# Unpinning the matmul engine's instruction order in a two-layer decoder trunk

## The chip, the cores and the metric

The kernel runs on one core of one Trainium2 chip. The metric is the device time of one execution in microseconds (us); smaller is better. The time before is the median of three runs.

## The reference

The reference is a trunk of two layers over 256 tokens of width 2048 in float32. Each layer computes

```
h = rms_norm(x, norm_mix);  proj = h @ w_in            # columns shared out among three groups of heads
A: 4 heads of differential attention (two softmax maps a head, subtracted, then an RMS norm per head)
B: 6 heads of softmax attention with a running forget gate added to the logits
C: 6 heads of latent attention (q and kv go through low-rank products first)
x = x + concat(A, B, C) @ w_out
x = x + square(relu(rms_norm(x, norm_ffn) @ w_ff_up)) @ w_ff_down      # 8192 wide
```

All heads are causal, with q and k normalised per head. With 256 tokens there are two blocks of 128 rows.

## The kernel before

**Weights.** Every weight matrix is streamed from HBM once, in tiles of 128 rows by up to 1024 columns. `load_w` loads a tile into `wraw` (5 buffers), ScalarE (ACT) rounds it to `whi` (3 buffers) and VectorE (DVE) computes the rest `wlo` (3 buffers). Each product is a sum of three: activation high part by `whi`, activation low part by `whi`, activation high part by `wlo`. TensorE (PE) accumulates it in PSUM. A weight tile therefore is a burst of matmuls: 8 on `whi` and 4 on `wlo` in a projection, for instance.

**Stages of a layer.** First come the projection groups `mq`, `mkv`, `fv0`, `fq0`, `fk0`, `fv1`, `fq1`, `fk1`, `dq`, `dk`, `dv` (with the low-rank products `qup` and `kvup` behind `mkv`), then the output product `wo`, then the feed-forward products `u` (up) and `dn` (down) in blocks of 1024 hidden columns.

**Attention in the background.** The attention of a head is a generator: scale q and k on DVE, transpose them on PE (`qk`), copy to SBUF, scores on PE (`s`), mask, exp and normalise on DVE and ACT (`p`), transpose the probabilities on PE (`pt`), copy (`pT`), weighted values on PE (`o`), split into `mix`. The object `bg` (`Background`) holds these generators, and after every weight tile `bg.step()` advances them by 1.25 stages on average. So attention is interleaved by hand with the next group's weight tiles. For the differential heads, `diff_rotation` scales and rotates `dqk` on DVE, `diff_maps` makes two maps and their difference, and `diff_outputs` normalises `osb` and transposes it into the last four slots of `mix`. The first 12 of the 16 rows of `mix` heads are multiplied by the left half of `w_out` while this runs; `bg.finish()` then runs what is left, and the last four heads follow.

**Order of the work.** The tile framework orders each engine's instructions at compile time. It walks a timing estimate of its own; on each engine it takes, of the instructions whose inputs that estimate says are there and whose buffers are free, the one that stands earliest in the program. The chip then runs each engine's list in that order, and semaphores make an instruction wait for its inputs. DVE, ACT and the DMA queues are ordered so. PE is the exception: `mm` and `transpose_block` hand every matmul and transpose to `in_order`, which ties it behind the PE instruction traced just before it. PE's list is the program's own order:

```
def in_order(ins):
    tc.keep_in_program_order(ins)
def mm(out, lhsT, rhs, start, stop):
    in_order(nc.tensor.matmul(out, lhsT, rhs, start=start, stop=stop))
def transpose_block(dst, src):
    in_order(nc.tensor.transpose(dst, src, ident))
```

Score, transpose and value tiles share four PSUM buffers (`t_tile`); the accumulators of the projections have four others (`acc_tile`). The feed-forward blocks use the two sets in turn.

Of the kernel before, what the change touches and what calls it, by code (L numbers as in the profile page):

```python
# [125 lines left out]
def trunk_kernel(ctx: ExitStack, tc: tile.TileContext, ins: dict, out: bass.AP):  # L126
    nc = tc.nc
# [12 lines left out]
    def t_tile(name):  # L140
        return ps_t.tile([P, 512], F32, tag="t", name=name)


    def in_order(ins):
        tc.keep_in_program_order(ins)

    def mm(out, lhsT, rhs, start, stop):
        in_order(nc.tensor.matmul(out, lhsT, rhs, start=start, stop=stop))  # L148

    bg = Background()  # L150

# [16 lines left out]
    for _ in range(WARM):  # L168
        mm(warm, zeros[:, :P], zeros, True, True)
# [8 lines left out]
    ident, ones, upto = (cst[:, i * P:(i + 1) * P] for i in range(3))  # L178
# [50 lines left out]
    class FirstNorm:  # L229
# [33 lines left out]
        def scale(self):  # L263

            b = t_tile("ss")
            for t in range(NT):
                for i in range(2):
                    mm(b[:, t:t + 1], self.squares[:, i * SEQ + t * P:i * SEQ + (t + 1) * P], ones[:, 0:1], i == 0, i == 1)
            ss = sp.tile([P, NT], F32, tag="ssm", name=f"ss_{self.name}")
            nc.vector.tensor_copy(ss, b[:, :NT])  # L270
            return rsqrt_of(ss, NT, [(slice(0, NT), D_MODEL)], self.name)

    class Norm:
# [7 lines left out]
        def columns(self, c0, n):  # L281
            for q in range(c0 // 512, (c0 + n) // 512):
                for t in range(NT):
                    junk = sp.tile([P, 512], F32, tag="junk", name="junk")
                    nc.scalar.activation(junk, x[:, t, q * 512:(q + 1) * 512], AF.Square, accum_out=self.sums[:, t, q:q + 1])
            for k in range(c0 // P, (c0 + n) // P, 2):
                b = acc_tile("xt")
                for i in range(2):
                    for t in range(NT):
                        transpose_block(b[:, i * SEQ + t * P:i * SEQ + (t + 1) * P], x[:, t, (k + i) * P:(k + i + 1) * P])  # L290
                h = parts_tile("ht", "ht")
                for i in range(2):
                    split_to(h[:, i], b[:, i * SEQ:(i + 1) * SEQ], self.gain[:, k + i:k + i + 1])
                self.h.append(h)
                yield
# [7 lines left out]
    def product_t(acc, chunks, hi, lo, off, start, stop):  # L303


        for w in (hi, lo):
            for i, (c, j) in enumerate(chunks):
                wk = w[:, off + i * P:off + (i + 1) * P]
                if w is hi:
                    mm(acc, wk, c[:, j].rearrange("p a t -> p (a t)"), start and i == 0, False)  # L310
                else:
                    mm(acc[:, :SEQ], wk, c[:, j, 0, :], False, stop and i == len(chunks) - 1)
# [43 lines left out]


    def transpose_block(dst, src):
        in_order(nc.tensor.transpose(dst, src, ident))

    def scores(q_terms, k_terms, decay=None):

# [26 lines left out]
    def transposed_p(p):  # L389

        pt = t_tile("pt")
        for i in range(3):
            transpose_block(pt[:, i * P:(i + 1) * P], p[:, i * P:(i + 1) * P])
        pT = ap.tile([P, 3 * P], F32, tag="pT", name="pT", bufs=3)
        nc.scalar.copy(pT, pt[:, :3 * P])
        return pT
# [8 lines left out]
    def heads_transposed(pairs):  # L405

        b = t_tile("qk")
        for i, blocks in enumerate(pairs):
            for t in range(NT):
                transpose_block(b[:, i * SEQ + t * P:i * SEQ + (t + 1) * P], blocks[t])  # L410
        return b
# [14 lines left out]
    for l in range(DEPTH):  # L426
# [85 lines left out]
        for g in range(4):  # L512
            dst = mk if g < 2 else mv
# [468 lines left out]
def build(shapes):  # L982
    import concourse.bacc as bacc

    nc = bacc.Bacc("TRN2", target_bir_lowering=False, num_devices=1, dynamic_dma_scratch_size=1024)
    ins = {k: nc.dram_tensor(f"in_{k}", s, F32, kind="ExternalInput").ap() for k, s in shapes.items()}
    out = nc.dram_tensor("out_0", (SEQ, D_MODEL), F32, kind="ExternalOutput").ap()
    with tile.TileContext(nc) as tc:  # L988
        trunk_kernel(tc, ins, out)
    return nc  # L990
# [9 lines left out]
```

## Time and profile before

| what | value |
|---|---|
| median of 3 runs | 2188.17 us (2185.26 to 2188.57) |
| time of the profiled execution | 2187.5 us |
| its span, first to last instruction | 2185.7 us |
| instructions | 29225, of these 11080 matmuls or transposes on PE |
| PE busy | 2158.2 us, 99% of the span |
| mean granted TensorE clock | 0.996 |

PE is the row for matmuls and transposes, PEld the row for the weight loads of the same engine, which overlap the matmuls before them. Matmuls are pipelined, and their ends are modelled; an idle time of PE in a row is counted from the modelled end of the one before. A granted clock of 1.00 is 2.4 GHz, 0.5 is 1.2 GHz.

### The profile page before, as it was taken

How to read it: one execution, taken by the hardware profiler on the slowest of the kernel's cores; microseconds unless marked ns; L12 is line 12 of the kernel's file. 1: busy time of each engine (PE TensorE's matmuls, PEld its weight loads, DVE VectorE, ACT ScalarE, POOL GpSimd, SP SyncE). 2: the span in 40 equal slices, each digit the busy share in tenths (PEclk: the TensorE clock that was granted, in tenths of full speed). 3: DMA queues.
4: the chain of work that ended last, by engine and by line, in shares of the span. 5: the costliest groups of instructions: out<-in, count | busy, mean ns of one | idle time of the engine just before them, and what ended most of it. 6: DMA issues, size and time to landing. Idle time of an engine off the chain costs nothing. (4 is left out here: it accounts for less than half of the span.)

```text
span 2185.7 us, 29225 instructions
## 1 busy us (share of the span) xinstructions
PE 2158.2 (99%) x11080; PEld 1864.3 (85%) x11080; DVE 1359.8 (62%) x2160; ACT 1085.4 (50%) x1603; POOL 12.7 (1%) x16
## 2 busy tenths in 40 slices
PE   9999999999999999999999999999999999999999
PEld 7998778888888888888889997788888888888887
DVE  7876656665565555655568766666565655655554
ACT  6655445554444444444456554555444544444442
POOL 2000000000000000000000000000000000000000
PEclk9999999999999999999999999999999999999999
DMA  8545435555556665565655455455565566566664
GB/s 270 175 139 170 151 132 165 191 185 193 190 193 190 190 191 192 191 193 183 187 161 169 142 177 164 137 182 186 190 192 193 188 192 190 191 192 193 190 191 149
DMA packets 115421, 395.70 MB, mean 181 GB/s; under 512 B 13008, under 2 KB 13136, under 8 KB 115280
## 3 DMA queue, kind: packets, MB, share of 16 engines
q1 hardware_dynamic: 115280, 393.83, 56.7%
q8 instruction: 87, 1.43, 0.3%
q14 instruction: 54, 0.44, 0.1%
HBM read 391.68 MB, written 2.10 MB: 180 GB/s over the span
## 5 line engine op out<-in xcount | busy, mean ns | idle before, releaser
L199 DVE TENSOR_TENSOR wlo<-wraw,whi 128x1024 fp32r<-128x1024 f32 (+3 forms) x773 | 908.6, 1177 | 727.9 <-ACT whi L198 717.6
L198 ACT ACTIVATE whi<-wraw 128x1024 fp32r<-128x1024 f32 (+3 forms) x773 | 789.7, 1023 | 968.7 <-PE dn L148 361.9
L148 PE MATMUL u<-ht,whi 128*128 128x512 f32 x2048 | 513.0, 392 | 0.0
L148 PE MATMUL dn<-whi,g 128*128 128x512 f32 x2048 | 511.2, 390 | 0.9 <-ACT whi L198 0.4
L148 PEld LDWEIGHTS dn<-whi,g 128*128 128x128 f32 x2048 | 383.0, 188 | 82.0 <-DVE x L327 2.3
L148 PEld LDWEIGHTS u<-ht,whi 128*128 128x128 f32 x2048 | 369.1, 189 | 66.7
L148 PEld LDWEIGHTS u<-ht,wlo 128*128 128x128 f32 x2048 | 279.4, 190 | 20.0
L148 PE MATMUL u<-ht,wlo 128*128 128x256 f32 x2048 | 285.5, 282 | 0.0
L148 PE MATMUL dn<-wlo,g 128*128 128x512 f32 x1024 | 276.3, 389 | 0.0
L148 PEld LDWEIGHTS dn<-wlo,g 128*128 128x128 f32 x1024 | 192.2, 188 | 40.0
L148 PE MATMUL wo<-whi,mix 128*128 128x512 f32 x512 | 138.8, 403 | 0.3
L148 PEld LDWEIGHTS wo<-whi,mix 128*128 128x128 f32 x512 | 95.3, 190 | 20.1 <-ACT mix L212 0.7
L327 DVE TENSOR_TENSOR x<-dn,x 128x512 f32<-128x512 f32 x128 | 79.7, 684 | 26.1 <-PE dn L148 26.1
L148 PE MATMUL wo<-wlo,mix 128*128 128x512 f32 x256 | 73.9, 390 | 0.0
L379 ACT ACTIVATE p<-p,nm 128x128 f32<-128x128 f32 x80 | 35.9, 450 | 44.2 <-DVE nm L378 44.2
L148 PEld LDWEIGHTS wo<-wlo,mix 128*128 128x128 f32 x256 | 48.3, 188 | 10.6
L831 DVE TENSOR_TENSOR relu<-u,relu 128x256 f32<-128x256 f32 x128 | 53.5, 418 | 0.0
L148 PE MATMUL fq<-whi,ht 128*128 128x384 f32 x256 | 52.9, 348 | 0.0
L148 PE MATMUL fk<-whi,ht 128*128 128x384 f32 x256 | 51.7, 343 | 0.0
L148 PE MATMUL fv<-whi,ht 128*128 128x384 f32 x256 | 51.0, 340 | 0.0
L830 ACT COPY relu<-u 128x256 f32<-128x256 f32 x128 | 46.0, 359 | 0.0
L832 DVE SCALAR_TENSOR_TENSOR relu<-relu,rsb 128x512 f32<-128x512 f32 x64 | 44.3, 692 | 2.3
(252 smaller groups left out, 1680.7 us busy)
## 6 DMA issues: line engine op xcount, KB each, us to landing
wraw<-in_w_up SPq DMA_DIRECT2D x256, 512.0 KB, 4.0
wraw<-in_w_down_a SPq DMA_DIRECT2D x128, 512.0 KB, 3.6
wraw<-in_w_down_b SPq DMA_DIRECT2D x112, 512.0 KB, 3.6
wraw<-in_w_out_a SPq DMA_DIRECT2D x32, 512.0 KB, 3.6
wraw<-in_w_out_b SPq DMA_DIRECT2D x32, 512.0 KB, 3.5
wraw<-in_w_fv SPq DMA_DIRECT2D x32, 384.0 KB, 3.1
wraw<-in_w_fq SPq DMA_DIRECT2D x32, 384.0 KB, 3.2
wraw<-in_w_fk SPq DMA_DIRECT2D x32, 384.0 KB, 3.1
```

The costliest lines, as they stand in the source:

```text
L148: in_order(nc.tensor.matmul(out, lhsT, rhs, start=start, stop=stop))
L198: nc.scalar.activation(hi[:, cols], raw[:, cols], AF.Copy)
L199: nc.vector.tensor_tensor(lo[:, cols], raw[:, cols], hi[:, cols], ALU.subtract)
L327: nc.vector.tensor_tensor(cols, acc, cols, ALU.add)
L379: nc.scalar.activation(p[:, cols], p[:, cols], AF.Exp, bias=nm[:, i:i + 1], scale=-1.0, accum_out=z[:, i:i + 1])
L830: nc.scalar.copy(r[:, cols], u[i][:, SEQ:])
L831: nc.vector.tensor_tensor(r[:, cols], u[i][:, :SEQ], r[:, cols], ALU.add)
L832: nc.vector.scalar_tensor_tensor(r, r, 0.0, rsb2, ALU.max, ALU.mult)
```

## The change

`in_order` is removed. `mm` and `transpose_block` issue the instruction and return; nothing else in the program's text is different. PE's list is then made as those of the other engines are: at each point the scheduler may take a later instruction that it holds to be ready before an earlier one that it holds not to be.

```
-
-    def in_order(ins):
-        tc.keep_in_program_order(ins)
-
     def mm(out, lhsT, rhs, start, stop):
-        in_order(nc.tensor.matmul(out, lhsT, rhs, start=start, stop=stop))
+        nc.tensor.matmul(out, lhsT, rhs, start=start, stop=stop)
...
     def transpose_block(dst, src):
-        in_order(nc.tensor.transpose(dst, src, ident))
+        nc.tensor.transpose(dst, src, ident)
```

## Rows read from the trace of the kernel before

**Rows 1.** Page, part 1: busy us (share of the span) xinstructions.
```profile
PE 2158.2 (99%) x11080; PEld 1864.3 (85%) x11080; DVE 1359.8 (62%) x2160; ACT 1085.4 (50%) x1603; POOL 12.7 (1%) x16
```

**Rows 2.** Windows: span; busy us of PE, PEld, DVE, ACT, POOL; PEclk, DMA share, GB/s.
```profile
440.00:1045.00 605.00, 605.00 (x3083) 517.21 (x3082) 355.88 (x387) 278.28 (x334) 0.00 (x0) 1.00 0.60 191
165.00:440.00 275.00, 264.10 (x1318) 223.20 (x1317) 172.22 (x339) 142.01 (x247) 0.00 (x0) 0.99 0.51 163
1155.00:1430.00 275.00, 270.28 (x1449) 243.08 (x1448) 194.00 (x484) 153.58 (x294) 0.00 (x0) 0.99 0.50 157
```

**Rows 3.** Windows of PE alone: span, PE busy, PEclk, DMA share, GB/s.
```profile
0.00:55.00 55.00, 49.78 (x244) 0.97 0.80 270
...
275.00:330.00 55.00, 50.17 (x230) 0.94 0.38 126
1320.00:1375.00 55.00, 52.91 (x239) 0.97 0.50 157
...
2145.00:2186.00 41.00, 35.87 (x159) 0.96 0.42 141
```

**Rows 4.** Waits of PE: who waited for whom, us in total, times, longest.
```profile
PE pt L359 <- DVE p L735: 5.9, 5, 2.5
PE qk L359 <- DVE dqk L421: 4.2, 2, 2.1
PE qk L359 <- DVE fqk L661: 2.1, 1, 2.1
...
PE dt L359 <- ACT qd L437: 1.5, 2, 1.3
PE fv L148 <- DVE wlo L199: 1.4, 3, 0.6
...
PE o L148 <- ACT pT L395: 1.1, 2, 0.6
PE qk L359 <- DVE osb L764: 0.5, 2, 0.3
```

**Rows 5.** Timeline of PE, layer 0, `dv`: start, us, instruction [idle before].
```profile
268.47 1.98 PE L148 MATMUL dv<-whi,ht 128*128 128x512 f32 x8
270.29 1.07 PE L148 MATMUL dv<-wlo,ht 128*128 128x512 f32 x4
271.20 0.27 PE L359 MATMUL qk<-cst,dqk 128*128 128x128 f32 x1
273.56 0.98 PE L359 MATMUL qk<-cst,dqk 128*128 128x128 f32 x7 [2.10 <-DVE dqk L421]
...
277.41 1.47 PE L148 MATMUL dv<-wlo,ht 128*128 128x512 f32 x4
```

**Rows 6.** Timeline of PE, layer 0, differential maps beside `wo`.
```profile
289.32 0.81 PE L148 MATMUL s<-kT,half 128*128 128x128 f32 x4
290.18 0.83 PE L359 MATMUL pt<-cst,p 128*128 128x128 f32 x3
293.49 0.83 PE L359 MATMUL pt<-cst,p 128*128 128x128 f32 x3 [2.48 <-DVE p L735]
...
315.65 3.64 PE L148 MATMUL wo<-whi,mix 128*128 128x512 f32 x8
...
320.65 2.09 PE L148 MATMUL wo<-whi,mix 128*128 128x512 f32 x8
```

**Rows 7.** Timeline of DVE, layer 0, between the two `pt` of rows 6.
```profile
290.43 0.28 DVE L378 CUSTOM_DVE_ANT_0 p<-s,cst 128x128 f32<-128x128 f32 x1
...
290.99 1.22 DVE L199 TENSOR_TENSOR wlo<-wraw,whi 128x1024 fp32r<-128x1024 f32 x1
...
293.35 0.48 DVE L736 SCALAR_TENSOR_TENSOR p<-p,r 128x256 f32<-128x256 f32 x1
```

**Rows 8.** Timeline of ACT, layer 0: the weight tiles being rounded.
```profile
267.77 1.06 ACT L198 ACTIVATE whi<-wraw 128x1024 fp32r<-128x1024 f32 x1 [1.66 <-PE dv L148]
270.49 1.06 ACT L198 ACTIVATE whi<-wraw 128x1024 fp32r<-128x1024 f32 x1 [1.66 <-PE dv L148]
...
288.72 1.04 ACT L198 ACTIVATE whi<-wraw 128x1024 fp32r<-128x1024 f32 x1
```

## The prediction

> **What bounds the kernel now.** I read the page's busy shares first: PE is busy for 2158.2 of 2185.7 us, DVE for 62%, ACT for 50% [rows 1]. So 27.5 us of idle PE is all that an order of PE's list can win directly. The windows show where it lies. From 440 to 1045 us, the feed-forward part of layer 0, PE has not one idle microsecond and DVE and ACT have 41% and 54% to spare [rows 2]; layer 1 has the same part. The two attention stretches hold the rest: 275.00 − 264.10 = 10.9 us in layer 0 and 275.00 − 270.28 = 4.7 us in layer 1 [rows 2].
>
> The list of PE's waits says what PE stood at there: transposes of probabilities waiting for DVE 5.9 us, transposes of rotated q and k 4.2, of forget-gate q and k 2.1, of the low-rank q 1.5, of the differential output 0.5, value products waiting for the copied probabilities 1.1, projection matmuls waiting for `wlo` 1.4 [rows 4]. Together 16.7 us. Of the remaining 10.8 us, 5.1 lie behind 2145 us, after PE's last matmul, and most of the rest in the first 55 us, which lack 5.2 (the 1.5 of the low-rank q among them) [rows 3]; nothing else is there to be run in either place.
>
> Such a wait costs more than itself. In layer 0 PE stands 2.10 us at the second `qk` transpose. The `wlo` burst of the next `dv` tile then takes 1.47 us where the one before took 1.07 [rows 5]; and after the `pt` waits, a `wo` burst of eight takes 3.64 us where its neighbour takes 2.09 [rows 6]. The granted clock is 0.94 in that window and 0.97 in the one of layer 1 that has the same `qk` wait [rows 3]: it fell to the lower level, 1.2 GHz, after PE had stood. What that costs follows from the clock column: 0.06 × 55 + 0.03 × 55 = 5.0 us.
>
> **The change part by part.** *Removed:* 11080 ordering ties [rows 1]. They are no instructions and cost nothing by themselves; no matmul, weight load, DMA or buffer is added or taken away. *Moved:* the places of PE's instructions among each other, and, since the scheduler places DVE and ACT work by the same estimate, some of theirs.
>
> What can fill a wait? At 271.2 us the next `dv` tile's weights have long been rounded: the tiles that ACT rounds at 267.77 and 270.49 us [rows 8] are the second and third burst from there (there are three `whi` buffers). At 291 us the same: the rounding at 288.72 is done [rows 8] when PE stands until 293.49 [rows 6]. One burst is 1.98 + 1.07 us less overlap [rows 5], more than any single wait. So work for each of these waits lies ready on the chip, and nothing has to be fetched for it.
>
> Will the scheduler see the wait? That needs its estimate to be late where the chip is. For the `pt` waits I think so, by structure: between the first and the second `pt` stands nothing on PE, while DVE must reduce, ACT exponentiate, and DVE scale and subtract, from 290.43 to 293.35 us plus the end of the last step [rows 7]; no estimate can make that chain nothing. The same holds for `osb`, whose transposes come directly behind the normalisation, and, less surely, for `dqk`, whose last rotation steps are dealt out one weight tile ahead. The clock loss hangs on the `dqk` and `pt` waits. The other four (`fqk` 2.1, `dt` 1.5, `o` 1.1, `fv` 1.4: 6.1 us) depend on a tight race, and there I cannot tell how the scheduler sees it; lower bound nothing, upper bound 6.1. I take nothing, since each is a single lateness that other places of the same kind do not show.
>
> Sum: 5.9 + 4.2 + 0.5 = 10.6 us of waits, plus 5.0 us of clock, 15.6 us. A passed transpose comes back only between two matmuls, and the scheduler's estimate will not hit the chip's moment. I leave one matmul at each of the nine waits (from 268.47 to 271.20 us there are twelve, 0.23 us each [rows 5]): 9 × 0.23 = 2.1 us kept. Gain 13.5 us, so 2187.5 − 13.5 = 2174.0 us. The profiled execution lies 0.7 us under the median of the runs shown, within their scatter, so I predict 2174. Bounds of this case alone: nothing of the open four and half of the rest gives −7.8, thus 2179.7; all of it gives −21.7, thus 2165.8.
>
> What is late next when the stall goes? The heads' own chain. PE is work-conserving: earlier instructions keep their priority, so a head comes later by at most the burst matmul in progress. Where the burst is taken early, its buffers are freed early and ACT and DVE refill sooner, with 38% and more of their time free [rows 1].
>
> In the feed-forward part I cost the edit at nothing. The cover is the absence of any wait: with the next matmul in program order always ready, the scheduler has no cause to pass it.
>
> One rule of the Trainium skill would draw another sum. "Perfetto Trace Analysis", section "Identifying the Most-Contended Engine", judges TensorE's headroom by the busy share of its weight loads and not by that of its matmuls. The loads are busy 85% [rows 1], and by that the order could free up to 15% of the span, an estimate of 1866 us. The trace does not bear this out: in the stretch without a wait the loads are idle for 87.8 of 605 us while matmuls run the whole time [rows 2], and every matmul brings its own load in either order.
>
> **Rivals.**
>
> *A, nothing happens.* The scheduler holds the late inputs for punctual, or sees the lateness elsewhere than the chip does; PE's list stays nearly the program's and the waits stay or trade places. For it: DVE's steps are short (0.28 to 0.48 us, [rows 7]), and a scheduler that prices them lower sees shorter chains. Against it: the chain between the two `pt`. Time 2187.5, give or take 3.
>
> *B, slower: burst matmuls pulled ahead of weights that are not there.* DVE's list shows what free order does: a `wlo` of 1.22 us is pushed into the middle of the softmax chain [rows 7], as the chain's next step was not ready at that instant. On PE a later tile's matmul may be put ahead of a transpose because the scheduler holds `whi` and `wlo` to be made, while the chip's ACT and DVE are behind. PE then stands at the matmul, with the transpose queued behind it, and the head's softmax behind that. Price per occurrence: one rounding and one remainder, 1.04 + 1.22 = 2.3 us [rows 7, 8]. Six such waits eat the 13.5 us; from eight on the kernel is slower by over 0.2%. With 12, and three falls of the clock at 5.0/3 = 1.7 us, it is 27.6 + 5.1 − 13.5 = 19 us slower: 2207. For it: the projections alone hold 2 × 11 × 8 = 176 weight tiles, by the code. Against it: the two or three tiles in advance.
>
> *C, all is won.* Scheduler and chip agree everywhere, the open four go as well, and the 2.1 us are not kept: 2187.5 − 21.7 = 2165.8.
>
> *D, the weight-load rule:* 1866 us, from headroom that the rows place inside the pipeline.
>
> **How the numbers follow.** Chances: the forecast (a partial gain, about 2166 to 2183) 0.52; C 0.09; A 0.20; B 0.18; D 0.01. A measurement of this kernel can tell about 0.2%, 4.4 us, from no change, so faster means under 2183.8 and slower over 2192.5. Faster are the forecast, C and D: 0.62. The same is A: 0.20. Slower is B: 0.18. The range takes in the forecast, C and A: it begins under C's time, at 2163, and ends at 2191, half a microsecond above A's 2190.5. Outside are B and D, 0.19. The forecast's own range is 2166 to 2180.
>
> **What would show it.** Right: in the changed profile PE's idle falls from 27.5 to about 15 us, the `pt` and `dqk` waits shrink to a few tenths each, bursts of `dv` and `wo` are split with transposes in their midst, and the windows near 275 and 1320 us show a clock of 1.00. The feed-forward stretch keeps PE fully busy with the same matmuls in the same order. Wrong, by A: the same waits in the same places. Wrong, by B: new PE waits for `whi` or `wlo` in the projection and `wo` bursts, or for `mix` ahead of the last four heads. Wrong in a way that I have not priced: idle PE in the feed-forward part.

## The result: 2163.36 us, 1.1% faster

The changed kernel takes 2163.36 us (median of 4 runs, 2162.75 to 2163.61), the kernel before 2187.63 us (4 runs): a ratio of 0.989, 95% interval 0.9873 to 0.9907. That is 24.3 us, against the 13.5 us that were forecast. The profiled execution took 2162.75 us with a span of 2161.0 us, 24.7 us shorter than the span before. Line numbers are 4 lower than before (L144 is L148, L355 is L359).

The page of the changed kernel, part 1, answers to [rows 1]; the windows under it, one over the feed-forward part and two over the attention stretches (columns as in [rows 2]), answer to that group:

```profile
PE 2147.7 (99%) x11080; PEld 1858.4 (86%) x11080; DVE 1358.7 (63%) x2160; ACT 1082.2 (50%) x1603; POOL 13.5 (1%) x16
```

```profile
435.00:1040.00 605.00, 604.80 (x3063) 516.14 (x3062) 354.64 (x384) 276.10 (x330) 0.00 (x0) 1.00 0.61 191
165.00:435.00 270.00, 268.24 (x1371) 228.34 (x1371) 178.19 (x345) 145.47 (x251) 0.00 (x0) 1.00 0.54 172
1140.00:1410.00 270.00, 268.44 (x1446) 241.00 (x1445) 194.00 (x481) 151.59 (x289) 0.00 (x0) 1.00 0.51 160
```

PE has the same 11080 instructions. It is idle for 2161.0 − 2147.7 = 13.3 us, where it was 27.5, and it is busy for 10.5 us less, which the same work at a clock that no longer falls explains in part. The attention stretches lack 1.8 and 1.6 us instead of 10.9 and 4.7.

The waits of PE in the changed kernel, beside [rows 4]:

```profile
PE mq L144 <- ACT whi L194: 1.6, 2, 0.9
...
PE mq L144 <- DVE wlo L195: 1.1, 1, 1.1
PE fv L144 <- DVE wlo L195: 0.8, 2, 0.4
PE qk L355 <- DVE dqk L417: 0.6, 2, 0.4
PE pt L355 <- DVE p L731: 0.6, 3, 0.2
PE wo L144 <- ACT mix L208: 0.5, 2, 0.2
...
PE dt L355 <- ACT qd L433: 0.4, 1, 0.4
PE qk L355 <- DVE osb L760: 0.3, 2, 0.2
PE qk L355 <- DVE fqk L657: 0.3, 1, 0.3
```

The 16.7 us of those seven are 3.0 now (the wait of `o` is no longer in the list). Two small ones are new or longer: `wo` for `mix`, 0.5 us, and `mq` for `wlo` at the start, 1.1 us for 0.2. PE's timeline in layer 0 shows how the late transposes are passed, first at the `dqk` transposes [rows 5], then at the two `pt` [rows 6]:

```profile
264.55 0.38 PE L355 MATMUL qk<-cst,dqk 128*128 128x128 f32 x2
264.68 1.87 PE L144 MATMUL dv<-whi,ht 128*128 128x512 f32 x7
266.91 0.87 PE L355 MATMUL qk<-cst,dqk 128*128 128x128 f32 x6 [0.36 <-DVE dqk L417]
267.54 0.48 PE L144 MATMUL dv<-whi,ht 128*128 128x512 f32 x1
267.86 1.09 PE L144 MATMUL dv<-wlo,ht 128*128 128x512 f32 x4
...
279.11 0.81 PE L144 MATMUL s<-kT,half 128*128 128x128 f32 x4
...
280.47 0.44 PE L355 MATMUL pt<-cst,p 128*128 128x128 f32 x2
280.67 1.87 PE L144 MATMUL wo<-whi,mix 128*128 128x512 f32 x7
282.37 1.07 PE L144 MATMUL wo<-wlo,mix 128*128 128x512 f32 x4
283.28 0.39 PE L144 MATMUL wo<-whi,mix 128*128 128x512 f32 x1
283.51 0.27 PE L355 MATMUL pt<-cst,p 128*128 128x128 f32 x1
```

Seven of the eight `dv` matmuls on `whi` stand where PE stood for 2.10 us, and twelve `wo` matmuls between the two `pt`. DVE's chain to the second `pt` is no shorter; its last step in the changed kernel begins 4.1 us after the scores at 279.11, where it was 4.0 us before (293.35 [rows 7] after 289.32 [rows 6]):

```profile
282.99 0.35 DVE L731 SCALAR_TENSOR_TENSOR p<-p,r 128x128 f32<-128x128 f32 x1
283.25 0.48 DVE L732 SCALAR_TENSOR_TENSOR p<-p,r 128x256 f32<-128x256 f32 x1
```

PE is what stopped waiting, DVE is not what became faster. The lists themselves differ little: by the operands that the two traces show, some 67 of the 11080 matmuls and transposes have to be moved to turn one list into the other. All but one of them lie at places that the table below names. Of the projections this is the stretch at `fqk`:

```
-qk<-cst,fqk 128x128 x4
 dq<-whi,ht 128x512 x8
+qk<-cst,fqk 128x128
 dq<-wlo,ht 128x512
+qk<-cst,fqk 128x128 x3
 dq<-wlo,ht 128x512 x3
```

**Where the 24.7 us are.** The start of one and the same burst in both timelines gives what the changed kernel leads by at that point; the difference from point to point is what the place between gave.

| burst behind the place | before | after | lead | the place gave |
|---|---|---|---|---|
| `mkv`, ahead of `dt` | 35.50 | 34.37 | 1.13 | 1.1 start |
| `mkv`, behind `dt` | 41.85 | 39.37 | 2.48 | 1.35 `dt` |
| `fq` on `wlo`, ahead of `pt` | 176.67 | 173.57 | 3.10 | 0.6 `fv` |
| `fq` on `wlo`, behind `o` | 180.97 | 177.09 | 3.88 | 0.8 `o` |
| `dq`, behind `fqk` | 211.97 | 206.09 | 5.88 | 2.0 `fqk` |
| `dk` on `wlo`, behind `o` | 240.36 | 233.71 | 6.65 | 0.8 `o` |
| first `wo` | 282.61 | 272.67 | 9.94 | 3.3 `dqk` |
| `wo`, behind the first two `pt` | 301.02 | 287.69 | 13.33 | 3.4 `pt` |
| `wo`, behind the next two `pt` | 320.65 | 303.24 | 17.41 | 4.1 `pt` |
| `wo`, behind `osb` | 337.99 | 320.54 | 17.45 | 0 `osb` |
| last `dn` block of layer 0 | 1060.30 | 1041.76 | 18.54 | 1.1 `dn` |
| `dv`, layer 1 | 1354.02 | 1335.36 | 18.66 | 0.1 |
| first `wo`, layer 1 | 1368.17 | 1346.08 | 22.09 | 3.4 `dqk` |
| `wo`, behind two `pt` | 1383.75 | 1360.99 | 22.76 | 0.7 `pt` |
| `wo`, behind two `pt` | 1403.62 | 1379.95 | 23.67 | 0.9 `pt` |
| last `dn` block of layer 1 | 2139.89 | 2115.16 | 24.73 | 1.1 `dn` |

The first row can't be put down to the order. Over all kernels of this document the `mkv` burst ahead of `dt` begins between 33.70 and 35.64 us where the matmuls are tied there, and between 33.96 and 35.77 where they are free. Only behind `dt` do they part: 41.43 us and later tied, 40.60 and earlier free.

### The profile page after: what moved, and what is told of

Read it like the earlier page. It is cut to its first block, busy times and chain, and to the rows that moved or that the text cites. A ratio compares the mean times of both kernels' runs of the same rounds, so it can differ in the third digit from the quotient of the medians.

```text
span 2161.0 us, 29221 instructions
## 1 busy us (share of the span) xinstructions
PE 2147.7 (99%) x11080; PEld 1858.4 (86%) x11080; DVE 1358.7 (63%) x2160; ACT 1082.2 (50%) x1603; POOL 13.5 (1%) x16
## 5 line engine op out<-in xcount | busy, mean ns | idle before, releaser
L144 PE MATMUL u<-ht,whi 128*128 128x512 f32 x2048 | 513.0, 392 | 0.0
L144 PE MATMUL dn<-whi,g 128*128 128x512 f32 x2048 | 510.5, 390 | 0.4 <-ACT whi L194 0.4
L144 PEld LDWEIGHTS dn<-whi,g 128*128 128x128 f32 x2048 | 383.1, 188 | 79.7 <-issue 1.2
L144 PEld LDWEIGHTS u<-ht,whi 128*128 128x128 f32 x2048 | 369.2, 189 | 66.7
L144 PEld LDWEIGHTS u<-ht,wlo 128*128 128x128 f32 x2048 | 279.4, 190 | 20.0
L144 PE MATMUL u<-ht,wlo 128*128 128x256 f32 x2048 | 285.5, 282 | 0.0
L144 PE MATMUL dn<-wlo,g 128*128 128x512 f32 x1024 | 277.3, 389 | 0.0
L144 PEld LDWEIGHTS dn<-wlo,g 128*128 128x128 f32 x1024 | 192.3, 188 | 40.0
L144 PE MATMUL wo<-whi,mix 128*128 128x512 f32 x512 | 138.1, 400 | 0.5 <-ACT mix L208 0.5
L144 PEld LDWEIGHTS wo<-whi,mix 128*128 128x128 f32 x512 | 94.3, 188 | 19.4 <-ACT mix L208 0.9
L144 PE MATMUL wo<-wlo,mix 128*128 128x512 f32 x256 | 74.1, 390 | 0.0
L144 PEld LDWEIGHTS wo<-wlo,mix 128*128 128x128 f32 x256 | 48.0, 188 | 10.4
L144 PE MATMUL fq<-whi,ht 128*128 128x384 f32 x256 | 53.7, 349 | 0.0
L144 PE MATMUL fk<-whi,ht 128*128 128x384 f32 x256 | 51.7, 343 | 0.0
L144 PE MATMUL fv<-whi,ht 128*128 128x384 f32 x256 | 51.1, 340 | 0.0
```

## The experiments

The edits are against the kernel before, unless it says otherwise; each ratio is to the kernel before in the same job, whose own median was 2186.0 to 2187.3 us there.

**Which half of the change does it.** First, matmuls free and transposes tied; then the reverse.

```
 def mm(out, lhsT, rhs, start, stop):
-    in_order(nc.tensor.matmul(out, lhsT, rhs, start=start, stop=stop))
+    nc.tensor.matmul(out, lhsT, rhs, start=start, stop=stop)
```

> Matmuls are free, transposes stay tied behind the PE instruction traced before them. Theory (burst matmuls pass late transposes and fill PE's waits): nearly the whole gain, 2163 to 2166 us, PE idle about 13 us, no fall of the clock after the start. Rival (the gain comes from transposes that are pulled forward to where they are ready): 2180 us or more, since a tied transpose can't go ahead of its predecessor.

Measured: 2163.81 us, ratio 0.9893 (0.9878 to 0.9907). The whole gain.

```
 def transpose_block(dst, src):
-    in_order(nc.tensor.transpose(dst, src, ident))
+    nc.tensor.transpose(dst, src, ident)
```

> Transposes are free, every matmul stays tied behind the PE instruction traced before it, a transpose too. Theory (burst matmuls pass late transposes): no gain, 2184 to 2190 us, the waits of pt, dqk and fqk stay within 1 us of before. Rival (transposes pulled forward): 2170 us or less.

Measured: 2185.26 us, ratio 0.9991 (0.9982 to 1.0000). These waits of PE stay:

```profile
PE pt L359 <- DVE p L735: 5.8, 5, 2.5
PE qk L359 <- DVE dqk L421: 4.0, 2, 2.0
PE qk L359 <- DVE fqk L661: 2.1, 1, 2.1
```

A transpose that may move alone moves only forward, and it was late already. What has to move is the matmul behind it. (Freed transposes do shorten one lesser wait, that of `fv`, from 1.4 to 0.8 us.)

**PE's order or that of the others.** The scheduler places DVE and ACT by the same estimate, so their lists changed too. In this kernel PE is free, and every DVE and ACT instruction is tied behind the one that preceded it in the list of the kernel before (code shortened; the DMA queues and POOL are not tied):

```
     (PE free, as in the changed kernel)
+    for before, after in zip(names, names[1:]):     # the recorded list of DVE, then of ACT
+        tc.add_manual_dep(traced[after], before, NoSync)
```

> PE is free as in the changed kernel, but the instructions of DVE and ACT are tied to each other in the order that they had in the kernel before. Theory (PE's own order makes the gain): 2162 to 2167 us. Rival (the gain comes from the changed order of DVE and ACT, which follow PE's): 2178 us or more.

Measured: 2166.36 us, ratio 0.9904 (0.9889 to 0.9919). So it saves 20.6 of the 2186.99 us of its own job with the old order of DVE and ACT. Of the other 3 us against the changed kernel, a part lies at the `osb` transposes, where PE now stands; behind that wait the clock falls in the profiled execution (0.58 from 321.5 to 325 us), and the next `wo` burst takes 3.41 us where it takes 2.11 in the changed kernel:

```profile
PE qk L359 <- DVE osb L764: 2.2, 3, 1.9
```

The profiled execution was the longest of the four (2168.20 us), so how the 3 us divide is open.

**Which stretch.** A flag turns `in_order` off up to the output product and on in the feed-forward part, and then the reverse.

```
+pinned = [False]     # True in the second kernel
 def in_order(ins):
-    tc.keep_in_program_order(ins)
+    if pinned[0]:
+        tc.keep_in_program_order(ins)
...
 bg.add(scale_rows())
+pinned[0] = True      # at the head of a layer: False; in the second kernel the other way round
```

> PE is free from the start of each layer to the end of the output product, tied in the feed-forward part. Theory (attention and projections hold the gain; the ends of the feed-forward part hold 1.0 us a layer): about 2165 us, 2163 to 2167. Rival (a good part lies in the feed-forward part, where free order mixes the matmuls of two tiles): 2172 us or more.

Measured: 2166.18 us, ratio 0.9903 (0.9888 to 0.9918), inside what was expected.

> The reverse: PE tied up to the output product, free in the feed-forward part. Theory: 2 us saved, at the last block of each layer alone; 2183 to 2188 us. Rival: 2175 us or less.

Measured: 2184.59 us, ratio 0.9991 (0.9981 to 1.0000): 2.4 us, at the edge of what can be told from nothing, and as large as the table's two `dn` rows together (2.2). What they are shows PE's timeline at the last `dn` block of layer 0, before, with what DVE does meanwhile, and then in the changed kernel:

```profile
1056.39 3.15 PE L148 MATMUL dn<-whi,g 128*128 128x512 f32 x8 [0.20 <-ACT whi L198]
1059.38 1.08 PE L148 MATMUL dn<-wlo,g 128*128 128x512 f32 x4
1060.30 1.99 PE L148 MATMUL dn<-whi,g 128*128 128x512 f32 x8
```

```profile
1055.55 2.48 DVE L327 TENSOR_TENSOR x<-dn,x 128x512 f32<-128x512 f32 x4 [0.63 <-PE dn L148]
```

```profile
1038.95 0.70 PE L144 MATMUL dn<-whi,g 128*128 128x512 f32 x2 [0.20 <-ACT whi L194]
1039.49 0.39 PE L144 MATMUL dn<-wlo,g 128*128 128x512 f32 x1
1039.72 0.62 PE L144 MATMUL dn<-whi,g 128*128 128x512 f32 x2
```

Before, the burst of eight walks through four accumulators while DVE is emptying them (four steps from 1055.55 us on); it takes 3.15 us in place of 1.99, at a granted clock of 1.00. Free, PE finishes all it can do on the first accumulator (two on `whi`, one on `wlo`) while the next is emptied. In the second kernel's own trace, where nothing else is free, the first two bursts of the block are split in the same way and take from 1058.33 to 1061.17 us, 2.84 in place of 3.91.

**What the falls of the clock cost.** Matmuls on a tile of zeros, whose results are overwritten or not used, fill three of the waits and shorten none.

```
 pt = t_tile("pt")
+for _ in range(fill):        # 14 before the fourth pt of layer 0
+    mm(pt[:, :SEQ], zeros[:, :P], zeros[:, :SEQ], True, True)
...
+if i == 0 and t == 1:        # 16 before the second dqk transpose of each layer
+    for _ in range(fill):
+        mm(b[:, SEQ:], zeros[:, :P], zeros[:, :SEQ], True, True)
```

> All tied as before. Extra matmuls on a tile of zeros, whose result is overwritten or not used, stand in front of three late transposes: 16 of 256 columns before the second dqk transpose of each layer, 14 before the second late pt of layer 0. They fill the wait and shorten nothing. Theory (the clock falls because PE stood, and each of the three falls costs 1.7 us): the granted clock stays at 1.00 after the start and the time drops by about 5 us to 2182 to 2184. Rival (the falls belong to something else, or cost nothing): 2187 us or above.

Measured: 2185.15 us, ratio 0.9991 (0.9982 to 1.0001): 1.9 us, not 5, and the interval does not exclude that nothing changed. The three falls are gone from its trace, but another one is there. PE's timeline of this kernel:

```profile
291.57 1.08 PE L359 MATMUL pt<-cst,p 128*128 128x128 f32 x3 [2.47 <-DVE p L740]
292.45 1.06 PE L359 MATMUL qk<-cst,dqk 128*128 128x128 f32 x4
293.16 3.03 PE L148 MATMUL wo<-whi,mix 128*128 128x512 f32 x8
```

This is the wait of 2.48 us in [rows 6], which was not filled. In the trace before, the clock did not fall after it, and the next `wo` burst took 2.08 us; here it fell (0.64 from 293 to 296 us), and the burst took 3.03. The kernel above that is tied up to the output product shows that the same list can do either. Its waits at `fqk` and `dqk` in layer 0 are those of the kernel before, but its clock fell behind `fqk` (0.66 from 210 to 215 us) and not behind `dqk` (1.00):

```profile
210.05 0.89 PE L362 MATMUL qk<-cst,fqk 128*128 128x128 f32 x4 [2.12 <-DVE fqk L665]
210.70 3.38 PE L151 MATMUL dq<-whi,ht 128*128 128x512 f32 x8
...
277.06 0.98 PE L362 MATMUL qk<-cst,dqk 128*128 128x128 f32 x7 [2.09 <-DVE dqk L424]
277.80 2.07 PE L151 MATMUL dv<-whi,ht 128*128 128x512 f32 x8
```

In the kernel before it was the other way round:

```profile
208.80 2.07 PE L148 MATMUL dq<-whi,ht 128*128 128x512 f32 x8
...
274.30 3.31 PE L148 MATMUL dv<-whi,ht 128*128 128x512 f32 x8
```

It fell behind `dt` as well (0.58 from 40 to 43 us), a wait of 1.5 us, where it did not fall in the kernel before. So the number and place of the falls are a matter of the execution, and all long waits have to be filled. The next kernel adds the other late `pt` of layer 0 (18 matmuls) and the late `fqk` transposes of layer 0 (16).

> All tied; extra matmuls on zeros now stand before all five waits of over 1.7 us: the dqk transposes of both layers, the two late pt of layer 0, and the first fqk transposes of layer 0. In the run with three filled the clock fell once at a wait that was not filled. Theory (which long wait brings the clock down differs from execution to execution, and each fall costs 1.7 us): with none left, no fall after the first 40 us, 2181 to 2184 us, and the executions lie within 2 us of each other where those of the kernel before spread over 3.4. Rival (the falls have another cause): falls remain and the spread stays.

Measured: 2182.72 us, ratio 0.9980 (0.9970 to 0.9989). Ten runs lie between 2182.46 and 2184.56 us, where 19 runs of the kernel before in the same job spread from 2184.22 to 2189.62. The windows of this kernel over both attention stretches show the clock at its upper level:

```profile
40.00:440.00 400.00, 395.16 (x2149) 1.00 0.51 166
1140.00:1440.00 300.00, 297.05 (x1604) 1.00 0.50 160
```

The fillers do no work for the result, so the 4.3 us (2.4 to 6.6 by the interval) are the price of the falls behind these five waits in a middling execution. Falls at the start and behind `dt`, which is not filled, remain possible. The remaining 20 us of the gain are the waits, the `dn` bursts (2.2) and the lead at the start.

**The same by hand.** The two `pt` follow each other because `diff_maps` ends without a `yield`, so that `side_by_side` goes on to the next generator in the same step. One line puts a weight tile between them, all else tied.

```
     dpT[i] = transposed_p(p1)
+    yield
```

> All tied as before, with one added yield at the end of diff_maps, so that the transposes of two maps no longer follow each other in one step but have a weight tile between them. Theory (the waits come from the program's bunching): the pt waits of 5.9 us fall under 1 us and about 9 us are saved where they were; but the chain of the differential heads ends later and the osb transposes come with no burst in front, which should cost 2 to 4 us a layer. Sum 2181 to 2186 us. Rival (the place in the list doesn't matter because DVE is the bound there): the waits only move, 2187 us or more.

Measured: 2190.69 us, ratio 1.0016 (1.0006 to 1.0025): not faster but slower by 3.6 us. The `pt` waits left the list, as expected; in their place stands one at `osb`, 5.2 us a layer where 2 to 4 had been allowed for, and the time lies where the rival had it, since the waits only moved:

```profile
PE qk L359 <- DVE osb L765: 10.4, 3, 5.2
```

The added stages push the heads' chain back, and at its end no burst is left. Does free order cover that one? The changed kernel with the same line:

> The changed kernel with the added yield that made the tied kernel slower: the differential heads end later, and the osb transposes have no weight burst in front of them. In the tied kernel that wait was 10.4 us in all. Theory (free order fills a wait only with matmuls whose inputs and buffers are there; before the last four heads every weight tile in the buffers belongs to products that themselves need those heads): the osb waits stay, about 8 to 11 us, and the time is 2168 to 2175 us. Rival (free order covers this wait too): 2162 to 2165 us.

Measured: 2176.00 us, ratio 0.9953 (0.9937 to 0.9970), 12.6 us slower than without the line, a microsecond beyond what was expected. The wait stays whole, and behind it the clock falls in both layers (0.79 from 318 to 326 us, 0.70 from 1395 to 1406):

```profile
PE qk L359 <- DVE osb L765: 10.1, 2, 5.2
```

That free order can't fill it is shown. That it can't because the buffered weight tiles all belong to the last four heads was argued only, not tried apart.

**How much work must lie ready.** Two buffers for `whi` and `wlo` in place of three, tied and then free:

```
-hi = wp.tile([P, 1024], F32R, tag="whi", name="whi", bufs=3)
-lo = wp.tile([P, 1024], F32R, tag="wlo", name="wlo", bufs=3)
+hi = wp.tile([P, 1024], F32R, tag="whi", name="whi", bufs=2)
+lo = wp.tile([P, 1024], F32R, tag="wlo", name="wlo", bufs=2)
```

> The kernel before with two buffers for whi and for wlo in place of three, so that less of the next weights is at hand. It is the base for the next run. I expect PE to wait for weights in many tiles: 2200 to 2400 us.

Measured: 2186.50 us, ratio 0.9997 (0.9987 to 1.0006). I was wrong: tied, the third buffer is worth nothing that these runs can tell.

> The changed kernel with two buffers for whi and for wlo. Theory (the tiles held ready ahead of PE are what fills the waits): the gain against the tied kernel with two buffers is under 20 us, since at a wait only one burst at most is ready. Rival (one burst is enough, or free order also hides the waits for weights): 24 us or more.

Measured: 2167.14 us, ratio 0.9910 (0.9895 to 0.9925), 19.4 us under the tied one. This is just under the line drawn, too near to it to decide by the total. The waits say more. A wait for the next tile's remainder has come in, which neither of the kernels with three buffers has; here tied and then free:

```profile
PE dv L148 <- DVE wlo L199: 3.5, 2, 1.7
```

```profile
PE dv L148 <- DVE wlo L199: 2.5, 2, 1.2
```

Tied, it stands in place of the `dqk` waits (4.2 us with three buffers, not in the list with two), and so the total is the same. Free, most of it stays, and the kernel is 3.8 us slower than with three buffers, in another job. That is in keeping with the theory, but doesn't single it out.

**Denser attention.** The changed kernel with `rate = 1.5` for 1.25:

> The changed kernel with attention advanced by 1.5 stages a weight tile in place of 1.25. Theory (late transposes are now passed, so bunching costs little, and heads that end sooner take away the waits before the last four heads, about 1 us a layer): 2160 to 2164 us. Rival (denser stages bring more late transposes than bursts can cover): 2166 us or more.

Measured: 2166.49 us, ratio 0.9906 (0.9891 to 0.9921), 3.1 us slower than the changed kernel, measured in another job. The rival held, by half a microsecond: waits for `fqk` of 2.5 us (0.3 in the changed kernel) have come in. None of the twelve beats the change as it is.

## Why the prediction was right, and where it was too small

**Direction and mechanism held.** Late transposes are passed by weight bursts, PE's idle time halves, the clock stays up. The signs that were named are there but for one: idle PE 13.3 us (15 forecast), `pt` and `dqk` at a few tenths each, bursts of `dv` and `wo` with transposes in their midst, a clock of 1.00 in the windows near 275 and 1320 us. The one that failed is that the feed-forward matmuls keep their order: at the last `dn` block of each layer they don't. Freeing the matmuls alone gives the whole gain (2163.81 us), it comes with the old order of DVE and ACT too (2166.36), and nearly all of it lies ahead of the feed-forward part (2166.18).

**The sum was too small by 11 us.** The time came out at rival C, which had a chance of 0.09, 2.4 us under C's sum and below the forecast's own range of 2166 to 2180. The stated range holds it by 0.4 us only, because its end was put under C and not because of a term that was worked out; so far it was luck. Three terms:

- "I take nothing" for the four open waits. They gave 1.35 + 0.6 + 1.6 + 2.0 = 5.5 us, with a bound of 6.1. The reason given, that each is a single lateness, was misread: by [rows 4] `dt` and `o` come twice and `fv` three times, and only `fqk` once. Nor does it say whether the scheduler sees a place as late; it did so at all four, though two of the three `fv` waits stay (0.8 of 1.4 us).
- The nine waits and the clock: 13.5 forecast, 15.8 measured (six rows of the table and `osb` at nothing). A matmul kept at each was a little too much: 1.5 us stay where 2.1 were left. The other 1.7 us are more than idle time (9.1 us less) and clock (5.0) explain. A wait costs more than the idle time that its row shows; why is not shown here.
- "Nothing" for the feed-forward part: 2.2 us. The cover was that the next matmul is always ready, read from the window that ends at 1045 us, ahead of the last `dn` block. That block loses 1.1 us a layer with hardly any idle time in the list of waits; only the length of its burst shows it, 3.15 us. (The 1.1 us of the start make up the rest of the 11 us; as said under the table, they can't be put down to the order.)

**The clock.** The 5.0 us were right for the profiled execution and were taken for a constant of the kernel. They are 4.3 us in a middling execution, and most of the difference between executions of the tied kernel goes with them: of the 64 beside the experiments, nine have a mean granted clock of 0.996 and a median of 2188.2 us, 32 have 0.998 and 2186.0.

**Rivals.** A fell: the scheduler sees the chip's late inputs as late. B fell, though two of its signs are there in small, both in the list above: `wo` waits for `mix` (0.5 us), and `mq` at the start for `wlo` (1.1 us, as much as in the kernel that is tied up to the output product). With two buffers `dv` waits for `wlo`, tied as well as free. D's time did not come near: the weight loads are still busy for 86%.

## What to carry to other kernels

Where an in-order engine is the bound and has other work buffered, look for its waits between instructions that follow each other directly in the program, and let the work behind pass, not the late instruction alone. The one spacing by hand that was tried moved the same work but lengthened the chain behind it (3.6 us lost, against 24.3 won). And price a wait by the burst behind it too: here its length showed accumulators still being emptied (3.15 us) and a fallen clock (3.31 and 3.64 us) where the same burst otherwise took 2.0 to 2.1, which idle time doesn't show.

## What was not expected of the hardware

After the same wait of 2.1 us, in the same place of the same list, the granted clock fell in one execution and not in another (bursts of 3.38 and 2.07 us at `fqk`, 2.07 and 3.31 at `dqk`). In another place, `dt`, it fell behind a wait of 1.5 us. With the five longest waits behind the start filled it did not fall between 40 and 440 us, nor between 1140 and 1440, and the kernel's runs moved together: 2.1 us of spread in ten runs, against 5.4 in nineteen.
